# A trunk layer on one core, with a block of unused products and element-wise instructions behind its last product

## The chip, the core and the metric

The kernel runs on one core of one Trainium2 chip. A core has five engines, each with its own instruction queue: TensorE (PE in the profile; its weight loads are shown apart as PEld), VectorE (DVE), ScalarE (ACT), GpSimd (POOL) and SyncE (SP), which here issues the transfers. Engines wait for each other through semaphores. TensorE writes to PSUM, of which there are eight banks of 512 fp32 columns; all other data of the core lie in SBUF.

The metric is the device time of one execution in microseconds, as the median of the runs. A profile, taken in an execution of its own, gives the start and the duration of each instruction; its times count from the first instruction, and its span ends with the last one.

## What is computed

One layer of a diffusion backbone, for 128 context tokens and 512 latent tokens with the same weights: normalisation and modulation, attention and a short convolution as mixers, and a convolutional feed-forward network. What concerns us is its last line:

```python
def conv_ffn(u, p):
    up = dwconv3(u @ p["w_up"], p["conv_ffn"])
    g, val = jnp.split(up, 2, axis=-1)
    return (jax.nn.silu(g) * val) @ p["w_down"]

def trunk_layer(h, ada, p, rope_tabs, ctx_k, ctx_v):
    ...
    u = rms_norm(h, p["g_pre2"]) * (1 + sc2) + sh2
    h = h + g2 * rms_norm(conv_ffn(u, p), p["g_post2"])
    return h, k, v
```

`w_down` has 2816 rows and 1024 columns. Everything is fp32.

## The kernel before

**Products.** An fp32 operand is split into two parts, `hi` (the value rounded to fp32r, the shorter format that TensorE takes at the full rate) and `lo` (what is left). ScalarE writes `hi` with a copy, VectorE writes `lo` with a subtraction. A product is then three products on TensorE, hi x hi, hi x lo and lo x hi, which add up in one PSUM bank. `mm3` (lines 235 to 237) issues the three.

**The end of the kernel.** The last product is that of the activations with the right half of `w_down`'s columns. Its rows are taken in pairs of 128 (index `p`). The latent tokens go by a scheme of Strassen's kind with seven block products for each pair, which are added up in seven banks (`accs[1]` to `accs[7]`, function `part`); the 128 context tokens go directly (function `context`, into `pms[0]`). For the last three pairs (`held`) the block products are put in another order: first 1, 5, 6, 7 of all three pairs, then 4, then 2, then 3, and last the context tokens. While TensorE still works on the later ones, VectorE combines the finished banks to output rows (`u2`, `u3`, `u4`, `C1`, `C2`), ScalarE sums their squares (`second_half`), GpSimd or VectorE makes the factor of the normalisation, and `stored` (line 2368) scales the rows, adds the input `h` and has SyncE store them. The context tokens are the last product and the last rows to be stored.

**Who sets the order.** In this part each engine takes its instructions in the order in which the code is written, and a recording layer adds the semaphore waits: for the writer of what is read, for the readers and the writer of what is overwritten. Room in SBUF goes by tags: `raw_tile()` gives the next of three rooms of 128 x 1024 fp32, and its first writer waits for the last readers of the tile that lay there.

**Names that the change uses.** `AR[0]` and `AR[1]` are rooms of fp32 activations, free at the end but for `p1`, `u2`, `u3` and `u4`. `AL` and `AH` hold the `lo` and `hi` parts of the activations in fp32r. `SR` and `TR` are two rooms of 1024 columns each in the tile `RAWS`. `JK` is a place for results that nobody reads, `ssqs` holds sums and factors of one column each. `state["raw"][base + NPAIR - 1]` is the last piece of `w_down` as it was loaded. Banks 3, 4, 5 and 6 held `accs[7]`, `accs[1]`, `accs[5]` and `accs[6]`.

Of the kernel before, what the change touches and what calls it, by code (L numbers as in the profile page):

```python
# [14 lines left out]
F16 = mybir.dt.float16  # L15
BF16 = mybir.dt.bfloat16
I32 = mybir.dt.int32
AF = mybir.ActivationFunctionType
ALU = mybir.AluOpType
# [93 lines left out]
def trunk_layer(ctx, tc, x_prompt, x_sample, cache_k, cache_v, c, c_ctx, w_ada, b_ada, g_pre1, g_post1, g_pre2,  # L113
# [3 lines left out]
    V, S, G, PE = nc.vector, nc.scalar, nc.gpsimd, nc.tensor  # L117
# [10 lines left out]
    def yrows(t):  # L128
        return y_prompt if t == 0 else y_sample[(t - 1) * 128:t * 128, :]
# [14 lines left out]
    def nm(s):  # L144
        cnt[0] += 1
        return f"{s}_{cnt[0]}"

    def region(pool, tag, shape, dtype, name):
        return pool.tile([128] + shape, dtype, tag=tag, name=name)
# [30 lines left out]
    state = {"next": 0, "raw": [], "cut": [], "limit": 10}  # L180

    def raw_tile():
        return wp.tile([128, 1024], F32, tag="raw", name=nm("raw"), bufs=3)
# [190 lines left out]
    with tc.tile_pool(name="pro", bufs=2) as pro, tc.manual_schedule(engines={mybir.EngineType.SP}):  # L374
# [216 lines left out]
        raw = state["raw"][0][:, 0:512]  # L591
# [41 lines left out]
        for f in range(2, KT):  # L633
# [32 lines left out]
            if f == KT - 3:  # L666
                V.tensor_scalar(out=gains[0], in0=gains[0], scalar1=HD ** -0.5, scalar2=None, op0=ALU.mult)
                for i in range(2):
                    for a in range(2):
                        V.tensor_tensor(out=tabs[i][:, :, 0, a * 32:a * 32 + 32], in0=rt[:, :, 0, a * 32:a * 32 + 32],  # L670
                                        in1=gains[i][:, :, a * 32:a * 32 + 32].broadcast_to((128, 4, 32)), op=ALU.mult)
                        for hf in range(2):
                            d0, s0 = a * 32 + hf * 16, a * 32 + (1 - hf) * 16
                            V.tensor_tensor(out=tabs[i][:, :, 1, d0:d0 + 16], in0=rt[:, :, 1, d0:d0 + 16],
                                            in1=gains[i][:, :, s0:s0 + 16].broadcast_to((128, 4, 16)), op=ALU.mult)
            if f == KT - 2:
# [9 lines left out]
                                op0=ALU.mult)  # L686
# [3 lines left out]
    AH = Halves(NTOK, F32R, "AH")  # L690
    AL = region(ra, "r3", [KT, NTOK], F32R, "AL")
# [22 lines left out]
    def work(name, eng, do, after=(), rooms=()):  # L714
        works.append(Work(name, eng, do, list(after), list(rooms)))
        return works[-1]
# [30 lines left out]
    with tc.tile_pool(name="att", bufs=1) as at:  # L747
# [11 lines left out]
        ssqs = at.tile([128, 4, 4], F32, name="ssqs")  # L759
# [140 lines left out]
        for t in range(NT):  # L900
# [30 lines left out]
            h = work(f"k{t} hi", "ACT", k_hi, [tk], [pk])  # L931
# [47 lines left out]
        for i in range(3):  # L979
            a = work(f"v hi {i}", "ACT",  # L980
                     lambda i=i: S.activation(VH[:, 0, 2 * i:2 * i + 2, :], rooms_v[i].tmp(), AF.Copy), scaled, [rooms_v[i]])
# [71 lines left out]
        for n, (g, t, pi) in enumerate(steps):  # L1053
# [52 lines left out]
            else:  # L1106
                pts[n], exs = [], []
                for h in hs:
# [16 lines left out]
                    if h:  # L1125
# [3 lines left out]
                                                                                   accum_out=mk[:, 4 + h:5 + h]), [mx], [ar[h]] + [er] * way)  # L1129
# [43 lines left out]
            if pi in (None, 1):  # L1173
# [20 lines left out]
                r = work(f"R{n}", "ACT", spread, list(pvs), [pvr, xr])  # L1194
                o = work(f"O{n}", "DVE", whole, [r], [pvr, xr])
                a = work(f"AH{n}", "ACT", ah, [o], [pvr])
# [50 lines left out]
    def bank(i):  # L1247
        if i >= 2 and len(pools) == 1:
            early.close()
            pools.append(ctx.enter_context(tc.tile_pool(name="pb", bufs=1, space=bass.MemoryType.PSUM)))  # L1250
        return pools[i >= 2].tile([128, 512], F32, tag=f"b{i}", name=nm(f"b{i}"))
# [289 lines left out]
    for m, (x, i) in enumerate(PAIRS):  # L1541
# [10 lines left out]
        e, o = 2 * before[1] if m else 0, 2 * before[1] + 1 if m else 0  # L1552
# [666 lines left out]
    NPAIR, NP0 = NJ // 2 - 2, 1  # L2219
    A0 = region(ra, "r0", [4, 2 * NACT], F32R, "A0")  # L2220
    A1 = region(ra, "r1", [4, 2 * NACT], F32R, "A1")
    AL, AH = [A0[:, i, :] for i in range(3)], [A0[:, 3, :], A1[:, 0, :], A1[:, 1, :]]
    T2 = A1.rearrange("p i c -> p (i c)")[:, 4 * NACT:4 * NACT + 2048]
    A2 = ra.tile([128, 2, 2 * NACT], F32, tag="r2a", name="A2")
    AR = [A2[:, i, :] for i in range(2)]
    EX = region(rb, "r4", [NT, D], F32, "EX")
    GJ = rb.tile([128, 2560], F32, tag="r5a", name="GJ")
    G2, JK = GJ[:, 0:2048].rearrange("p (r c) -> p r c", r=2), GJ[:, 2048:2560]
    RAWS = rb.tile([128, 2560], F32, tag="r5b", name="RAWS")
    SR, TR, C22 = RAWS[:, 0:1024], RAWS[:, 1024:2048], RAWS[:, 2048:2560]  # L2230
    SS, TS = {}, {2: T2}
    ssqs = sm_.tile([128, NT, 2], F32, name="ssqs", bufs=1)
# [75 lines left out]
    def part(p, n):  # L2308

        u, x, y = state["cut"][base + p], s_room(p), t_room(p)  # L2310
        l, r = {1: lambda: (share(p, NACT + X1), u.at(1, 0, 256)), 2: lambda: (share(p, X1), u.at(0, 0, 256)),
                3: lambda: (summed(x, 3), u.at(0, 256, 256)), 4: lambda: (share(p, X2), summed(y, 3)),
                5: lambda: (summed(x, 0), summed(y, 1)), 6: lambda: (summed(x, 2), summed(y, 2)),
                7: lambda: (summed(x, 1), summed(y, 0))}[n]()
        if n not in accs:
            accs[n] = bank({1: DBANKS[2], 5: DBANKS[3], 6: DBANKS[4], 7: DBANKS[1]}[n])
        for t in range(2):
            ts = slice(t * 128, t * 128 + 128)
            mm3(accs[n][:, t * 256:t * 256 + 256], l[0][:, ts], l[1][:, ts], *r, p == NP0 and t == 0 and n in (1, 5, 6, 7), p == NPAIR - 1 and t == 1)
# [23 lines left out]
    def halves_of(x):  # L2343
        return x.rearrange("p (i c) -> p i c", i=2)

    def second_half(t, src):
        row = 1 if t == 0 else 0
        first, second = ssqs[:, t, 0:1], ssqs[:, t, 1:2]
        S.activation(halves_of(JK), src, AF.Square, accum_out=second)  # L2349
        if t == 0:  # L2350
            V.tensor_tensor(out=EX[:, t, 512:1024], in0=pms[0], in1=G2[:, row, 512:1024], op=ALU.mult)
            S.activation(second, second, AF.Sqrt, bias=first)
            V.reciprocal(second, second)
        else:
            G.tensor_tensor(out=second, in0=second, in1=first, op=ALU.add)  # L2355
            G.tensor_tensor(out=second, in0=second, in1=mhalf[:, 0:1], op=ALU.pow)
# [7 lines left out]
    def stored(t, n=1):  # L2364
        r = ssqs[:, t, 1:2]
        for i in range(n):
            cs = slice(i * D // n, (i + 1) * D // n)
            V.scalar_tensor_tensor(out=EX[:, t, cs], in0=EX[:, t, cs], scalar=r, in1=room["h"][:, t, cs], op0=ALU.mult, op1=ALU.add)
            nc.sync.dma_start(yrows(t)[:, cs], EX[:, t, cs])
# [22 lines left out]
    w, x, y = NJ - 3, NJ - 2, NJ - 1  # L2392
# [30 lines left out]
    base = state["next"]  # L2423
# [35 lines left out]
    for p in held:  # L2459
        if p + 2 < NPAIR:  # L2460
            prepared(p + 2)
        for n in (1, 5, 6, 7):
            part(p, n)
    S.activation(ssqs[:, 0, 1:2], mhalf[:, 0:1], AF.Sqrt, scale=-1.0)
    p1, u2, u3, u4 = (AR[i // 2 % 2][:, i % 2 * 512:i % 2 * 512 + 512] for i in (2, 3, 0, 1))
    S.activation(p1, accs[1], AF.Copy)
    minus(C22, C22, accs[5])
# [24 lines left out]
        stored(t, 2)  # L2492
    second_half(0, halves_of(pms[0]))
    stored(0, 2)
    fixed.close()


# [27 lines left out]
```

## Time and profile before

| | us |
|---|---|
| median of 2 runs | 1075.42 |
| the runs | 1075.06 and 1075.78 |
| span of the profiled execution | 1073.0 |
| TensorE busy in it | 1056.8 |
| VectorE busy | 899.9 |
| ScalarE busy | 598.4 |
| GpSimd busy | 133.1 |

The profiled execution has no time of its own beside its span; the two runs were taken apart from it. A busy time is the time in which an engine had at least one instruction under way. Instructions of one engine can overlap in the profile (a product is shown with its whole way through the array), so how many of a kind fit into a stretch is read from the distance of their starts.

Rows of the timeline read: start in us, duration in us, engine, line of the kernel, operation, output<-inputs, shapes, and xN where N equal instructions in a row are merged (their duration is then from the first start to the last end). Idle time ahead of an instruction stands in brackets with what ended it. Rows by line or by name read: count, then duration in ns as minimum/median/maximum, or busy us and mean ns.

### The profile page before, as it was taken

What the parts mean: (1) busy time and instruction counts of PE and PEld (TensorE: products, weight loads), DVE (VectorE), ACT (ScalarE), POOL (GpSimd) and SP (SyncE); (2) the same over time, 40 slices, a digit from 0 to 9 for tenths busy, and PEclk for the clock granted to TensorE, in tenths of its full rate; (3) what the DMA queues carried; (4) which work ended last, traced back from release to release, by engine and by line L of the source; (5) the groups of instructions that cost most, each with busy time, mean ns of one, the idle gap of its engine ahead of it and who ended that gap; (6) DMA issues with size and microseconds to landing.
All of it is one profiled execution on the core that took longest, in us unless ns stands there. A gap on an engine that the chain in (4) does not pass through costs nothing.

```text
span 1073.0 us, 20652 instructions
## 1 busy us (share of the span) xinstructions
PE 1056.8 (98%) x8216; PEld 995.4 (93%) x8216; DVE 899.9 (84%) x1379; ACT 598.4 (56%) x1057; POOL 133.1 (12%) x162
## 2 busy tenths in 40 slices
PE   8999999999999999999999999999999999999997
PEld 6788898899999999999998789999999999999996
DVE  5699999865498999896599678889999988989897
ACT  5478999942344544445322366645555555546673
POOL 1087676500000000000000020000000000000001
PEclk9999999999999999999999999999999999999999
DMA  9829999962244333223668634434544534436873
GB/s 320 256 82 175 190 168 187 191 147 60 75 123 124 93 103 94 79 79 99 189 188 253 198 131 129 121 116 136 166 131 152 150 122 131 152 116 219 277 275 115
DMA packets 243197, 164.02 MB, mean 153 GB/s; under 512 B 94874, under 2 KB 216214, under 8 KB 243102
## 3 DMA queue, kind: packets, MB, share of 16 engines
q1 hardware_dynamic: 242990, 162.68, 55.5%
q8 instruction: 64, 1.05, 0.4%
q14 instruction: 31, 0.25, 0.1%
q10 hardware_dynamic: 112, 0.04, 0.0%
HBM read 123.31 MB, written 17.36 MB: 131 GB/s over the span
## 4 chain that ended last, share of the span: by engine, by line
PE 90%; DVE 3%; ACT 2%; DMA 1%; POOL 1%; issue 1%; SPq 1%; DVEq 0%; ACTq 0%; POOLq 0%
PE b L1274 47%; PE b L235 10%; PE b L237 10%; PE b L236 9%; PE s L709 4%; PE s L1073 2%; PE s L1170 2%; PE s L235 1%; PE s L237 1%; PE s L1162 1%; PE s L478 1%; DVE marks L1120 1%; PE s L236 1%; PE b L1900 1%; ACT P L1134 1%
## 5 line engine op out<-in xcount | busy, mean ns | idle before, releaser
L1274 PE MATMUL b<-ZBr,whi 128*128 128x320 f32 x688 | 152.1, 309 | 0.0
L1274 PE MATMUL b<-MT,whi 128*128 128x320 f32 x608 | 134.4, 309 | 0.0
L1274 PEld LDWEIGHTS b<-ZBr,whi 128*128 128x128 f32 x688 | 114.9, 188 | 0.1
L1274 PE MATMUL b<-ZBr,wlo 128*128 128x320 f32 x344 | 106.1, 308 | 0.0
L1274 PEld LDWEIGHTS b<-MT,whi 128*128 128x128 f32 x608 | 101.7, 188 | 0.0
L1274 PE MATMUL b<-MT,wlo 128*128 128x320 f32 x304 | 94.0, 309 | 0.0
L1261 ACT ACTIVATE whi<-SUM 128x1024 fp32r<-128x1024 f32 x40 | 42.2, 1055 | 78.3 <-DVE SUM L1813 75.7
L1843 DVE SCALAR_TENSOR_TENSOR Y<-C,cffn,Y 128x642 f32<-128x642 f32 x88 | 77.9, 886 | 0.9
L1261 ACT ACTIVATE whi<-WB 128x1024 fp32r<-128x1024 f32 x38 | 40.2, 1058 | 55.5 <-DVE WB L1368 55.5
L1274 PE MATMUL b<-ZBT,whi 128*128 128x320 f32 x320 | 71.0, 308 | 0.0
L1274 PE MATMUL b<-UL,whi 128*128 128x320 f32 x228 | 70.8, 311 | 0.0
L1274 PE MATMUL b<-UH,wlo 128*128 128x320 f32 x228 | 70.1, 307 | 0.0
L1274 PE MATMUL b<-UH,whi 128*128 128x320 f32 x228 | 69.7, 306 | 0.0
L1282 ACT ACTIVATE p<-b 128x320 f32<-128x320 f32 x78 | 34.1, 437 | 55.3 <-PE b L1274 53.5
L1274 PEld LDWEIGHTS b<-ZBr,wlo 128*128 128x128 f32 x344 | 64.6, 188 | 0.0
L1265 DVE TENSOR_TENSOR wlo<-raw,whi 128x1024 fp32r<-128x1024 f32 (+1 forms) x51 | 50.4, 1020 | 13.4 <-ACT whi L1261 13.4
L1274 PEld LDWEIGHTS b<-MT,wlo 128*128 128x128 f32 x304 | 57.1, 188 | 0.0
L1274 PEld LDWEIGHTS b<-ZBT,whi 128*128 128x128 f32 x320 | 54.2, 188 | 1.6
L1120 DVE TENSOR_REDUCE marks<-s 128x1 f32<-128x640 f32 x64 | 52.1, 817 | 4.0 <-PE s L1073 3.8
L1265 DVE TENSOR_TENSOR wlo<-WB,whi 128x1024 fp32r<-128x1024 f32 x38 | 46.5, 1224 | 8.8 <-ACT whi L1261 8.7
L2355 POOL TENSOR_TENSOR ssqs<-ssqs 128x1 f32<-128x1 f32 x4 | 1.4, 356 | 412.9 <-ACT GJ L2349 412.9
L1261 ACT ACTIVATE whi<-raw 128x1024 fp32r<-128x1024 f32 (+1 forms) x51 | 43.5, 892 | 15.4 <-DMA raw<-in_w_o_dram 12.5
(477 smaller groups left out, 3348.1 us busy)
## 6 DMA issues: line engine op xcount, KB each, us to landing
raw<-in_w_in_dram SPq DMA_DIRECT2D x48, 512.0 KB
RAW<-in_w_up_dram SPq DMA_DIRECT2D x40, 512.0 KB
raw<-in_w_down_dram SPq DMA_DIRECT2D x22, 512.0 KB
GA<-in_w_ada_dram SPq DMA_DIRECT2D x16, 512.0 KB
actd<-Y SPq DMA_DIRECT2D x18, 321.0 KB
actl<-ACTb SPq DMA_DIRECT2D x18, 321.0 KB
A<-actl SPq DMA_DIRECT2D x9, 642.0 KB
A<-actd SPq DMA_DIRECT2D x9, 642.0 KB
```

Of the source, the lines that this page charges most:

```text
L235: PE.matmul(out, ah, bh, start=start, stop=False)
L236: PE.matmul(out, ah, bl, start=False, stop=False)
L237: PE.matmul(out, al, bh, start=False, stop=stop)
L709: PE.matmul(out, a, b, start=start and n == 0, stop=stop and n == 2, skip_group_check=True)
L1073: PE.matmul(o[h], q_of(hl, i, rows), kk[kx][rows, g, ks], start=m == 0, stop=m == 2, tile_position=(64 * h, 0), skip_group_check=True)
L1120: V.tensor_reduce(out=mk[:, h:h + 1], in_=s_of(), axis=AX.X, op=ALU.max, negate=True)
L1170: PE.matmul(p[64 * h:64 * h + 64, i * 128:i * 128 + 128], VH[:, w, s, vc_], src, start=k == 0 and m == 0, stop=k == ks[-1][0] and m == 2, ...
L1261: S.activation(to[0], raw, AF.Copy)
L1265: V.tensor_tensor(out=lo, in0=raw, in1=hi.bitcast(F32), op=ALU.subtract)
L1274: PE.matmul(out, p[:, ws], q[:, k, :], start=start and k == 0 and n == 0, stop=stop and k == 3 and n == 2, skip_group_check=True)
L1282: S.activation(t, pair[j][b], AF.Copy)
L1843: V.scalar_tensor_tensor(out=y, in0=crows(j)[i][:, d:d + NACT], scalar=cffn[:, 44 * d + o:44 * d + o + 1], in1=y, op0=ALU.mult, op1=ALU.add)
```

## The change

A block is added that computes nothing for the outputs.

Behind the first part of the held pairs, ScalarE fills a new tile of 16-bit numbers, `H16` (a `raw_tile()` seen as 2048 fp16 columns), with two copies of the last piece of `w_down`, scaled by 64.

Behind the last `stored`, TensorE gets 288 products, each written alone (`start` and `stop`) into one of four banks in turn:

- 168 fp16 products with weights and moving operand from `H16`: 48 of 320 columns, 24 of 512, 24 of 256, 30 of 160, 30 of 128 and 12 of 320 (the loops run `count // 3` times over three products)
- 48 fp32r products on `AL` and `AH`: 24 of 320 columns, 12 of 512, 12 of 256
- 48 fp16 products of 320 columns on half the array's rows, the two halves in alternation
- 24 fp32r products of the same kind

Then VectorE gets 25 instructions of 128 x 1024 elements on fp32 inputs, all but one with 16-bit results in `H16[:, 0:1024]`: four subtractions, four scaled subtractions, one subtraction into `SR` (fp32), twelve subtractions, and four multiplications by a factor per row. GpSimd gets four fp32 additions of `SR` into `TR`, beside the twelve subtractions. ScalarE gets three squares of 512 elements with a sum, and six copies of 1024 elements into `H16[:, 0:1024]`, three of them with a factor read from `ssqs`.

```diff
     S.activation(ssqs[:, 0, 1:2], mhalf[:, 0:1], AF.Sqrt, scale=-1.0)
+    H16 = raw_tile().bitcast(F16)
+    for i in range(2):
+        S.activation(H16[:, 1024 * i:1024 * i + 1024], state["raw"][base + NPAIR - 1], AF.Copy, scale=64.0)
     p1, u2, u3, u4 = (AR[i // 2 % 2][:, i % 2 * 512:i % 2 * 512 + 512] for i in (2, 3, 0, 1))
     S.activation(p1, accs[1], AF.Copy)
...
     second_half(0, halves_of(pms[0]))
     stored(0, 2)
+    pbank = [bank(b) for b in (4, 5, 6, 3)]
+    turns = [0]
+
+    def pmm(l, r, n, rows=None, x=None):
+        o = pbank[turns[0] % 4] if x is None else pbank[x]
+        turns[0] += 1
+        PE.matmul(o[:, 0:n], l, r, start=True, stop=True, skip_group_check=True, **({} if rows is None else dict(tile_position=(rows, 0))))
+
+    for n, count in ((320, 48), (512, 24), (256, 24), (160, 32), (128, 32), (320, 12)):
+        for i in range(count // 3):
+            w = [H16[:, (2 * i + a) % 4 * 128:(2 * i + a) % 4 * 128 + 128] for a in range(2)]
+            y = [H16[:, 512 + 512 * a:512 + 512 * a + n] for a in range(2)]
+            for a, c in ((0, 0), (0, 1), (1, 0)):
+                pmm(w[a], y[c], n)
+    for n, count in ((320, 24), (512, 12), (256, 12)):
+        for i in range(count // 3):
+            w = [AL[a][:, (2 * i + a) % 4 * 128:(2 * i + a) % 4 * 128 + 128] for a in range(2)]
+            y = [AH[a][:, 0:n] for a in range(2)]
+            for a, c in ((0, 0), (0, 1), (1, 0)):
+                pmm(w[a], y[c], n)
+    for i in range(24):
+        for h in range(2):
+            rows = slice(64 * h, 64 * h + 64)
+            pmm(H16[rows, i % 4 * 128:i % 4 * 128 + 128], H16[rows, 512:832], 320, 64 * h, 2 * (i // 3 % 2) + h)
+    for i in range(12):
+        for h in range(2):
+            rows = slice(64 * h, 64 * h + 64)
+            pmm(AL[0][rows, i % 4 * 128:i % 4 * 128 + 128], AH[0][rows, 0:320], 320, 64 * h, 2 * (i // 3 % 2) + h)
+    a0, a1 = AR[0][:, 0:1024], AR[1][:, 0:1024]
+    for i in range(4):
+        V.tensor_tensor(out=H16[:, 0:1024], in0=a0, in1=a1, op=ALU.subtract)
+    for i in range(4):
+        V.scalar_tensor_tensor(out=H16[:, 0:1024], in0=a0, scalar=ssqs[:, 0, 1:2], in1=a1, op0=ALU.mult, op1=ALU.subtract)
+    V.tensor_tensor(out=SR, in0=a0, in1=a1, op=ALU.subtract)
+    for i in range(4):
+        G.tensor_tensor(out=TR, in0=a0, in1=SR, op=ALU.add)
+    for i in range(12):
+        V.tensor_tensor(out=H16[:, 0:1024], in0=a0, in1=a1, op=ALU.subtract)
+    for i in range(4):
+        V.tensor_scalar(out=H16[:, 0:1024], in0=a0, scalar1=ssqs[:, 0, 1:2], scalar2=None, op0=ALU.mult)
+    for i in range(3):
+        S.activation(JK, a0[:, 0:512], AF.Square, accum_out=ssqs[:, 3, 0:1])
+    for i in range(3):
+        S.activation(H16[:, 0:1024], a0, AF.Copy)
+    for i in range(3):
+        S.activation(H16[:, 0:1024], a0, AF.Copy, scale=ssqs[:, 0, 1:2])
     fixed.close()
```

How the instructions then stand on the engines is shown at three places. The first is ScalarE behind the last split of the held pairs, where `raw_11853` is the new tile `H16`, `raw_11683` the loaded weights, `A` the room of `p1` and `b` the bank of `accs[1]`.

```order
 L2464 ACT_TABLE_LOAD
 L2464 ACTIVATE ssqs<-mhalf 128x1
-L2466 ACTIVATE A_11085<-b_895_11427 128x512 [waits PE_49,Activation_49]
+L2467 ACTIVATE raw_11853<-raw_11683 128x1024 [waits Activation_49]
+L2467 ACTIVATE raw_11853<-raw_11683 128x1024
+L2469 ACTIVATE A_11085<-b_895_11427 128x512 [waits PE_49,Activation_49]
 L2349 ACTIVATE GJ,ssqs<-RAWS 128x512 [waits DVE_49]
```

The two copies into `H16` stand ahead of the copy of `accs[1]`; the names in brackets are the engines whose semaphore is waited for.

The second is TensorE from the last product of the context tokens on, in the kernel with the change.

```order
L235 MATMUL b_877_11090<-whi_11765,A_11084 128x512
L236 MATMUL b_877_11090<-wlo_11766,A_11084 128x512
L237 MATMUL b_877_11090<-whi_11765,A_11083 128x512
L2504 LDWEIGHTS raw_11853 [waits Activation_49]
L2504 MATMUL b_916_11975<-raw_11853 128x320 [waits Activation_49]
L2504 LDWEIGHTS raw_11853 [waits DVE_49]
L2504 MATMUL b_917_11976<-raw_11853 128x320 [waits PE_49]
L2504 LDWEIGHTS raw_11853
L2504 MATMUL b_918_11977<-raw_11853 128x320 [waits PE_49]
```

The new products follow directly; an fp16 product has its weight load as an instruction of its own, and the waits are for the copies into `H16` and for the last readers and writers of the four banks.

The third is VectorE at the end of the program.

```order
 L2368 SCALAR_TENSOR_TENSOR EX<-EX,ssqs,HX 128x512 [waits DVE_49]
 L2368 SCALAR_TENSOR_TENSOR EX<-EX,ssqs,HX 128x512
-L2521 UNCONDITIONAL_BRANCH
+L2528 TENSOR_TENSOR raw_11853<-A_11085 128x1024 [waits PE_49]
+L2528 TENSOR_TENSOR raw_11853<-A_11085 128x1024 [waits DVE_49] x3
+L2530 SCALAR_TENSOR_TENSOR raw_11853<-A_11085,ssqs 128x1024 [waits DVE_49] x4
+L2531 TENSOR_TENSOR RAWS<-A_11085 128x1024
+L2535 TENSOR_TENSOR raw_11853<-A_11085 128x1024 [waits DVE_49] x12
+L2537 TENSOR_SCALAR raw_11853<-A_11085,ssqs 128x1024 [waits DVE_49] x4
+L2570 UNCONDITIONAL_BRANCH
```

The first subtraction waits for TensorE, that is for the last reader of `H16` among the products, and each one that writes `H16` waits for the one ahead of it. On ScalarE the first of the six copies into `H16` waits for VectorE's last multiplication in the same way; on GpSimd the first addition waits for the subtraction into `SR`, and each further one for the addition ahead of it. SyncE's queue has the same transfers as before.

## The prediction

> **What bounds the kernel now.** I read the busy shares and the clock first, then the timeline of the last 12 us, then the closing barrier, and then the rows from which each kind of added instruction can be priced.
>
> On the page, a busy share stands behind each engine, and the clock line has one digit for each fortieth of the span.
>
> ```profile
> PE 1056.8 (98%) x8216; PEld 995.4 (93%) x8216; DVE 899.9 (84%) x1379; ACT 598.4 (56%) x1057; POOL 133.1 (12%) x162
> PEclk9999999999999999999999999999999999999999
> ```
>
> TensorE is busy from end to end at the full clock, so whatever stands behind its last product starts when that product ends. The timeline of the end (start in us, duration in us, engine, line) shows that moment and what follows it.
>
> ```profile
> 1065.33 0.39 PE L236 MATMUL b<-wlo,A 128*128 128x512 f32 x1
> 1065.56 0.39 PE L237 MATMUL b<-whi,A 128*128 128x512 f32 x1
> 1067.61 0.68 DVE L2351 TENSOR_TENSOR EX<-b,GJ 128x512 f32<-128x512 f32 x1
> 1068.21 0.15 DVE L2353 RECIPROCAL ssqs<-ssqs 128x1 f32<-128x1 f32 x1
> 1068.39 1.42 DVE L2368 SCALAR_TENSOR_TENSOR EX<-EX,ssqs,HX 128x512 f32<-128x512 f32 x2
> ```
>
> The next product could start at 1065.56 + 0.23 = 1065.8 us, 0.23 us being the distance of the two rows. VectorE is done at 1069.8 us. Behind that lie the last store and a barrier of all engines, here by line, with the first and last start:
>
> ```profile
> L2521 SPq DRAIN  x3: 7/7/13, 1072.2 to 1072.5; - x3
> L2521 POOLq EVENT_SEMAPHORE  x4: 17/17/17, 1072.3 to 1072.9; - x4
> ```
>
> SyncE is the last to arrive, at 1072.2 us, and the span ends at 1073.0: 0.8 us from the last arrival to the end, whoever is last. The span is 1073.0 us; the two runs took 1075.06 and 1075.78 us, so 2.4 us of their median of 1075.42 lie around the span. I keep these 2.4 us and add only what the span grows by.
>
> **What the change puts on the path.** The added work is one chain over three engines. TensorE does 216 products that read the new 16-bit tile H16 (and 48 on fp32r operands among them). The first new subtraction of VectorE overwrites H16, so it waits for the last fp16 product; the 24 fp32r half-row products behind that are beside it (1.8 us at 0.147 a pair, below, if they were not). Each VectorE instruction that writes H16 waits for the one before. ScalarE's six copies write the same part of H16, so they wait for all of VectorE's. The three products, subtractions and copies thus add up, and nothing is left of the old kernel that could hide them: its stores are over by 1072.2 us, some 25 us before TensorE is through. No result is stored, so no DMA is added.
>
> **TensorE.** A product's price in a stream is the distance to the next one, not its duration.
>
> ```profile
> 63.55 0.82 PE L947 MATMUL s<-P,some 128*128 128x256 bf16 x6
> L947 PEld LDWEIGHTS <-some x6: 98/98/98, 63.4 to 64.0; 128*128 128x128 bf16 x6
> L947 PE MATMUL s<-P,some x6: 272/272/273, 63.6 to 64.1; 128*128 128x256 bf16 x6
> 634.50 0.60 PE L1748 MATMUL b<-ident,TX 128*128 128x128 f32 x4
> L1748 PEld LDWEIGHTS b<-ident,TX x40: 138/140/145, 620.4 to 648.8; 128*128 128x128 f32 x40
> 329.83 0.31 PE L1274 MATMUL b<-MT,whi 128*128 128x320 f32 x1
> ...
> 330.86 0.31 PE L1274 MATMUL b<-MT,wlo 128*128 128x320 f32 x1
> 1061.38 0.28 PE L236 MATMUL b<-wlo,SS 128*128 128x256 f32 x1
> 1061.50 0.28 PE L237 MATMUL b<-whi,SS 128*128 128x256 f32 x1
> 84.40 0.31 PE L1073 MATMUL s<-KL,QT 64*128 64x320 f32 x2
> 84.55 0.46 PE L1073 MATMUL s<-KH,QT 64*128 64x320 f32 x4
> 84.84 0.31 PE L1073 MATMUL s<-KL,QT 64*128 64x320 f32 x2
> ```
>
> The kernel has no fp16 product over the whole array, but six bf16 ones of 256 columns, each with its own weight load like the new ones: (0.82 - 0.27) / 5 = 0.110 us apart. fp32r products of 256 columns are 0.12 us apart, those of 320 columns 1.03 / 7 = 0.147 us (seven steps between the two rows), those of 512 columns 0.23. Taking the bf16 row by columns, fp16 costs 0.1375 us at 320 columns and 0.220 at 512: 60 x 0.1375 + 24 x 0.220 + 24 x 0.110 = 16.2 us.
>
> For the 30 products of 160 and the 30 of 128 columns the columns alone would give 0.069 and 0.055 us, and then the weight load may be the limit. The f32 products of 128 columns are (0.60 - 0.27) / 3 = 0.109 us apart although their columns need half of that, so there the load is the limit. A 16-bit load is shown 42 ns shorter than an f32 one (98 against 140 ns). I take 0.109 - 0.042 = 0.067 us as its limit: 30 x 0.069 + 30 x 0.067 = 4.1 us, between 3.7 (columns alone) and 6.5 us (the f32 limit).
>
> On such loads the Trainium skill says two things. "TensorE: Matmul & The Clock Gate", in its section LDWEIGHTS, gives columns divided by 1.2 GHz, 107 ns for 128 columns, and by it the 60 narrow products would cost 6.4 us and the total 2.3 us more; a whole bf16 load shown with 98 ns speaks against it. The section on fast weight load of the same page has 16-bit loads of 128 columns at about twice the speed, and the shorter bf16 load of this trace agrees in direction.
>
> The 48 fp32r products cost 24 x 0.147 + 12 x 0.23 + 12 x 0.12 = 7.7 us. The 48 fp16 half-row products run as pairs: the trace has such pairs (each x2) 0.44 / 3 = 0.147 us apart, so 24 x 0.147 = 3.5 us. Sum: 16.2 + 4.1 + 7.7 + 3.5 = 31.5 us, until 1097.3. The last product ends 0.31 us after its start and not 0.147, which with a signal makes 1097.5 us. If fp16 were as slow as fp32r at every width, it would be 60 x 0.0095 + 24 x 0.011 + 24 x 0.010 + 2.4 = 3.5 us more.
>
> **VectorE.** These rows give its instructions of 1024 elements, and one that writes 16-bit results.
>
> ```profile
> L2261 DVE TENSOR_TENSOR SS<-RAWS,SS x8: 1217/1221/1231, 1009.3 to 1051.0; 128x1024 fp32r<-128x1024 f32 x8
> L1141 DVE SCALAR_TENSOR_TENSOR P<-s,P 128x640 f16<-128x640 f32 x32 | 26.2, 820 | 2.7 <-ACT P L1134 2.4
> L342 DVE SCALAR_TENSOR_TENSOR GA<-GA,s,GA x28: 1276/1280/1285, 532.9 to 601.6; 128x1024 f32<-128x1024 f32 x28
> L440 DVE TENSOR_SCALAR xn<-XT,rstd x5: 744/753/753, 6.8 to 13.3; 128x1024 f32<-128x1024 f32 x5
> ```
>
> A 16-bit result gains nothing: 0.82 us for 640 elements would be 1.31 for 1024, not less than the 1.22 of a 32-bit one. I take 1.22, since a fixed part is in the 0.82. A wait for the instruction before adds about 0.035 us (RECIPROCAL above ends at 1068.36, the next starts at 1068.39). So 17 subtractions x 1.255 = 21.3, 4 scaled subtractions x 1.315 = 5.3, 4 multiplications x 0.79 = 3.1: 29.7 us alone. The multiplications have twice the rate in the row, with a 32-bit result; if that is lost, 4 x 0.47 = 1.9 us come on top.
>
> **GpSimd beside it.** Its four additions of 1024 elements meet the last twelve subtractions. Two places in the trace show such a meeting; the lines of L831 give the undisturbed and the longest case.
>
> ```profile
> L831 POOL TENSOR_TENSOR wlo<-raw,whi x13: 1271/1289/1805, 71.2 to 193.6; 128x512 fp32r<-128x512 f32 x13
> L831 DVE TENSOR_TENSOR wlo<-raw,whi x5: 681/693/1221, 112.0 to 189.8; 128x512 fp32r<-128x512 f32 x5
> 112.01 1.82 DVE L831 TENSOR_TENSOR wlo<-raw,whi 128x512 fp32r<-128x512 f32 x2
> 112.24 1.04 POOL L870 TENSOR_TENSOR QF<-QF,X 128x256 f32<-128x256 f32 x1 [0.18 <-DVE QF L850]
> 152.37 0.69 DVE L831 TENSOR_TENSOR wlo<-raw,whi 128x512 fp32r<-128x512 f32 x1
> 152.41 1.80 POOL L831 TENSOR_TENSOR wlo<-raw,whi 128x512 fp32r<-128x512 f32 x1 [2.19 <-ACT whi L826]
> L1139 POOL TENSOR_TENSOR P<-E,P 128x640 f16<-128x640 f32 x29 | 40.8, 1408 | 30.3 <-ACT P L1134 30.2
> ```
>
> At 152.4 us VectorE started first; GpSimd's instruction ended 1.15 us after VectorE's (154.21 against 153.06), nearly its whole undisturbed 1.29. At 112 us GpSimd's ended at 113.28, and VectorE's second subtraction, which takes 0.69 undisturbed, was stretched to 1.22 and ended at 113.83, 0.55 us behind it. So two such instructions take turns, and a turn saves 0.14 us on either side. In the new block VectorE leaves a gap of 0.035 us between two subtractions, in which a waiting addition gets its turn, and each addition waits for the one before, so VectorE goes ahead once in between: four turns. An addition of 1024 elements is 2.25 us by the 1.41 of 640 elements and 2.58 by the 1.29 of 512; I take 2.4. Four turns cost VectorE 4 x (2.4 - 0.28) = 8.5 us, between 0 (no turns) and 9.2 (2.58 each). The additions end within the twelve subtractions. The Trainium skill, "SBUF — State Buffer", section on who interferes with whom, calls this an exclusive lock in which the loser fully blocks; both places above agree. VectorE's part: 29.7 + 8.5 = 38.2 us, until 1135.7.
>
> **ScalarE.** The three squares of 512 elements follow its last old instruction and are hidden under TensorE's 31 us (uncovered, at least 3 x 0.60 us, as the 512 elements at 1053.33 below). The six copies come last.
>
> ```profile
> 1049.53 1.04 ACT L2258 ACTIVATE SS<-RAWS 128x1024 fp32r<-128x1024 f32 x1
> L1134 ACT ACTIVATE P<-E x29: 728/738/780, 80.5 to 209.6; 128x640 f16<-128x640 f32 x29
> L1838 ACT ACTIVATE Y<-C,cffn x44: 816/830/842, 681.7 to 985.7; 128x642 f32<-128x642 f32 x44
> 1051.88 0.20 ACT L2464 ACTIVATE ssqs<-mhalf 128x1 f32<-128x1 f32 x1
> 1053.33 0.60 ACT L2466 ACTIVATE A<-b 128x512 f32<-128x512 f32 x1 [1.25 <-PE b L237]
> 1054.77 0.69 DVE L1288 TENSOR_TENSOR A<-A,b 128x512 f32<-128x512 f32 x1
> ```
>
> A copy takes 1.05 us; one with a scale read from SBUF about 0.1 us more (0.83 against 0.74 at some 640 elements). With 0.04 us for each wait: 3 x 1.09 + 3 x 1.19 = 6.8 us, and 0.1 us for the signal: until 1142.6. The two copies that fill H16 stand ahead of the copy of accs[1] (1053.33). They take 2.1 us from 1052.1, so that copy starts at 1054.2 and ends at 1054.8, when the subtraction that reads it starts (1054.77). That costs under 0.1 us, and TensorE waits for none of it.
>
> **Sum.** 1142.6 + 0.8 = 1143.4 us of span, 70.4 more than 1073.0. With the median of the runs: 1075.4 + 70.4 = 1146 us, slower by 6.5%.
>
> **The rivals.**
> - *No turns.* GpSimd's additions cost VectorE nothing, because they run beside it or wait until it is through. The first gives 1146 - 8.5 = 1137 us. In the second the additions (9.6 us) run beside the copies (6.8 us) and end 2.8 us later: 1140 us. For it: the two places have single meetings, none has a train of them. Against it: both show the later one waiting.
> - *Dearer instructions.* fp16 no faster than fp32r (+3.5), no double rate with a 16-bit result (+1.9), longer additions (+0.7), 1.31 us for a 16-bit subtraction (17 x 0.09 = +1.5): up to 1153 us. The bf16 row and the weight-load rows speak against the largest of these.
> - *Not slower.* The results are read by nobody, and if the build drops instructions without a reader, nothing but the copies into H16 and no time is left: 1075 us. It decides from the point where less than 28.7 us stand behind the last product (within 2% is up to 1073.0 + 21.5 = 1094.5 us of span). The rows of the changed program have all 288 products, so I give it next to nothing; even if all engines worked side by side without the chain, TensorE's 33 us would pass that point.
>
> **Chances.** The sum as worked out 0.65, no turns 0.18, dearer 0.15, not slower 0.02. The likeliest is 1146 us. The range runs from the lowest rival of the slower side, 1137 less 1 for narrow products at the rate of their columns, to 1152, where most of the dearer case is inside. A measurement of this kernel can tell about 2% from no change; every case but the last is 5 to 7% slower, so 0.98 slower, 0.01 the same, 0.01 faster.
>
> **What the changed profile would show.** TensorE's new line starts at 1065.8 and its fp16 parts end near 1097.5; VectorE's first subtraction waits for TensorE there. If the turns are right, four of the twelve subtractions are some 2 us longer than the others and GpSimd's additions are spread over the first five or six of them; if not, all twelve are 1.22 us. The last instruction is a copy of ScalarE, and the span ends 0.8 us behind it. Wrong would be: narrow products at 0.11 us, multiplications at 1.22 us, or a VectorE that starts long before TensorE's fp16 parts are through.

## The result, and the profile after

The kernel with the block takes 1143.93 us (median of 2 runs, 1143.71 and 1144.16) against 1075.42 us before: 1.064 times as long, with a 95% interval of 1.061 to 1.067. The profiled execution has a span of 1141.9 us, 68.9 us more than the 1073.0 before; the median lies 2.0 us above it.

The busy shares on the page of the kernel after:

```profile
PE 1089.5 (95%) x8504; PEld 1020.8 (89%) x8504; DVE 936.5 (82%) x1404; ACT 609.2 (53%) x1071; POOL 146.1 (13%) x166
```

TensorE has 288 products more (8504 against 8216), and unlike before it is not busy to the end. The timeline of the kernel after, from the old kernel's last product on (start in us, duration in us, engine, line; xN are merged):

```profile
1065.36 0.39 PE L237 MATMUL b<-whi,A 128*128 128x512 f32 x1
1065.59 19.87 PE L2504 MATMUL b<-raw 128*128 128x320 f16 x168
...
1085.19 0.42 PE L2504 MATMUL b<-A 128*128 128x320 f32 x1
1085.45 0.31 PE L2504 MATMUL b<-A,A 128*128 128x320 f32 x1
...
1087.19 0.31 PE L2504 MATMUL b<-A,A 128*128 128x320 f32 x1
...
1093.10 3.43 PE L2504 MATMUL b<-raw 64*128 64x320 f16 x48
1096.26 2.03 PE L2504 MATMUL b<-A 64*128 64x320 f32 x24
1096.57 5.01 DVE L2528 TENSOR_TENSOR raw<-A 128x1024 f16<-128x1024 f32 x4 [26.96 <-PE b L2504]
1101.61 5.25 DVE L2530 SCALAR_TENSOR_TENSOR raw<-A,ssqs 128x1024 f16<-128x1024 f32 x4
1106.78 1.22 DVE L2531 TENSOR_TENSOR RAWS<-A 128x1024 f32<-128x1024 f32 x1
1107.91 23.15 DVE L2535 TENSOR_TENSOR raw<-A 128x1024 f16<-128x1024 f32 x12
1108.13 13.04 POOL L2533 TENSOR_TENSOR RAWS<-A,RAWS 128x1024 f32<-128x1024 f32 x4 [42.22 <-issue]
1131.10 3.12 DVE L2537 TENSOR_SCALAR raw<-A,ssqs 128x1024 f16<-128x1024 f32 x4
1134.31 3.23 ACT L2541 ACTIVATE raw<-A 128x1024 f16<-128x1024 f32 x3 [65.33 <-DVE raw L2537]
1137.57 3.51 ACT L2543 ACTIVATE raw<-A,ssqs 128x1024 f16<-128x1024 f32 x3
```

It is one staircase: each engine starts where the one ahead of it is done. VectorE had been idle for 26.96 us when the last fp16 product let it go, and ScalarE for 65.33 us when VectorE did. GpSimd's additions start 0.2 us behind the first of the twelve subtractions. The end of the program is the same as before, 0.8 us from the last arrival to the end; here ScalarE's last copy ends at 1141.08 and the barrier's events of GpSimd run to

```profile
L2570 POOLq EVENT_SEMAPHORE  x4: 17/17/17, 1141.3 to 1141.8; - x4
```

The terms of the sum, in us:

| | forecast | measured |
|---|---|---|
| first new product | 1065.8 | 1065.6 |
| 168 fp16 products | 20.3 | 19.60 (1065.59 to 1085.19) |
| 48 fp32r products | 7.7 | 7.91 (to 1093.10) |
| 48 fp16 half-row products | 3.5 | 3.16 (to 1096.26) |
| VectorE's first subtraction | 1097.5 | 1096.57 |
| VectorE's part | 38.2 | 37.65 (to 1134.22) |
| ScalarE's copies, with the signal | 6.9 | 6.86 (to 1141.08) |
| to the end of the span | 0.8 | 0.8 |

Two boundaries in this table need care. These rows of TensorE are the last fp16 products ahead of the fp32r ones, the last fp32r product, and forty of the half-row products (twenty pairs):

```profile
1084.89 0.57 PE L2504 MATMUL b<-raw 128*128 128x320 f16 x3
1092.88 0.28 PE L2504 MATMUL b<-A 128*128 128x256 f32 x1
1093.38 2.88 PE L2504 MATMUL b<-raw 64*128 64x320 f16 x40
```

The last fp16 product starts at 1084.89 + 2 x 0.135 = 1085.16, so the first fp32r product is shown only 0.03 us behind it and the second another 0.26 us later: together the 0.28 us of an fp16 and an fp32r step. Some 0.1 us of the 7.91 thus belong to the 19.60. In the same way the last half-row pair is followed after 0.03 us by the next product, so the 3.16 us hold one step less than the 24 pairs. Within the row the pairs are (2.88 - 0.30) / 19 = 0.136 us apart, 0.30 us being the last product's duration.

The chain that ended last, in order of time, shows the twelve subtractions one by one (start, time on the chain; the first six are printed):

```profile
1107.99 1.15 DVE raw L2535
1109.17 3.26 DVE raw L2535
1112.45 3.26 DVE raw L2535
1115.72 3.26 DVE raw L2535
1119.00 3.25 DVE raw L2535
1122.28 1.24 DVE raw L2535
```

The second to the fifth take 3.26 us and all behind them 1.24: four turns of 2.02 us, as long as GpSimd has additions left. The durations by line say the same from both sides (count, minimum/median/maximum in ns):

```profile
L2535 DVE TENSOR_TENSOR raw<-A x12: 1219/1226/3246, 1107.9 to 1129.8; 128x1024 f16<-128x1024 f32 x12
L2533 POOL TENSOR_TENSOR RAWS<-A,RAWS x4: 3198/3200/3202, 1108.1 to 1118.0; 128x1024 f32<-128x1024 f32 x4
```

### The profile page after: what moved, and what is told of

It reads as the page before. It is cut to its first block, busy times and chain, and to the rows that moved or that the text cites. A ratio compares the mean times of both kernels' runs of the same rounds, so it can differ in the third digit from the quotient of the medians.

```text
span 1141.9 us, 21273 instructions
## 1 busy us (share of the span) xinstructions
PE 1089.5 (95%) x8504; PEld 1020.8 (89%) x8504; DVE 936.5 (82%) x1404; ACT 609.2 (53%) x1071; POOL 146.1 (13%) x166
## 4 chain that ended last, share of the span: by engine, by line
PE 90%; DVE 5%; ACT 2%; POOL 1%; DMA 1%; issue 1%; SPq 0%; ACTq 0%; DVEq 0%; POOLq 0%
PE b L1274 45%; PE b L235 9%; PE b L237 9%; PE b L236 9%; PE s L709 4%; PE b L2504 3%; PE s L1073 3%; PE s L1170 2%; DVE raw L2535 2%; PE s L1162 1%; PE s L235 1%; PE s L237 1%; PE s L478 1%; PE s L236 1%; PE b L1900 1%
```

## The experiments

The theory was a chain TensorE, VectorE, ScalarE that adds up, with turns between VectorE and GpSimd. The rivals were that VectorE is held or stretched by something else. All changes are made to the kernel after. The old part of the kernel ended up to 0.8 us earlier or later from one execution to the next (the first new product started between 1065.6 and 1066.4 us), so parts of the block are compared by their lengths where it matters: from VectorE's first subtraction to ScalarE's last copy, 44.51 us in the kernel after (1096.57 to 1141.08).

**Without the additions.**

```diff
-    for i in range(4):
-        G.tensor_tensor(out=TR, in0=a0, in1=SR, op=ALU.add)
```

> The four additions of GpSimd are left out. Turns theory (an addition and a subtraction with both inputs in SBUF exclude each other, each addition stretches one subtraction from 1.22 to 3.25 us): all twelve subtractions take 1.22 us and the span falls by 4 x 2.02 = 8.1 us, from 1141.9 to 1133.8 us. Rival (the long subtractions come from something else, as the waits of VectorE on itself or the 16-bit results): four of the twelve stay at 3.25 us and the span at 1141.9 us.

Measured: 1135.79 us, span 1134.1 us. The twelve subtractions by line, with the shortest, the middle and the longest in ns:

```profile
L2533 DVE TENSOR_TENSOR raw<-A x12: 1219/1224/1226, 1108.2 to 1122.1; 128x1024 f16<-128x1024 f32 x12
```

The first piece of the block in the timeline, VectorE's last and ScalarE's last (start and length in us):

```profile
1096.88 5.00 DVE L2528 TENSOR_TENSOR raw<-A 128x1024 f16<-128x1024 f32 x4 [26.96 <-PE b L2504]
...
1123.32 3.12 DVE L2535 TENSOR_SCALAR raw<-A,ssqs 128x1024 f16<-128x1024 f32 x4
...
1129.79 3.51 ACT L2541 ACTIVATE raw<-A,ssqs 128x1024 f16<-128x1024 f32 x3
```

Not one subtraction is over 1.226 us. The part from 1096.88 to 1133.30 is 36.42 us, 8.09 less than with the additions. So the long subtractions are the additions' doing, and the rival falls.

**Eight additions.**

```diff
-    for i in range(4):
+    for i in range(8):
         G.tensor_tensor(out=TR, in0=a0, in1=SR, op=ALU.add)
```

> Eight additions of GpSimd instead of four. Turns theory: eight of the twelve subtractions take 3.25 us, one addition between each two, and the span grows by 4 x 2.02 = 8.1 us to 1150.0 us. Rival (VectorE wins the later meetings and keeps going): the subtractions behind the fifth stay at 1.22 us, the last additions end beside ScalarE's copies, and the span stays within 3 us of 1141.9 us.

Measured: 1152.27 us, span 1150.9 us. The median of the subtractions is now the long one. The rows by line, then the first and the last piece of the block in the timeline:

```profile
L2535 DVE TENSOR_TENSOR raw<-A x12: 1216/3245/3247, 1108.8 to 1138.8; 128x1024 f16<-128x1024 f32 x12
L2533 POOL TENSOR_TENSOR RAWS<-A,RAWS x8: 3196/3201/3204, 1109.0 to 1131.9; 128x1024 f32<-128x1024 f32 x8
```

```profile
1097.41 5.01 DVE L2528 TENSOR_TENSOR raw<-A 128x1024 f16<-128x1024 f32 x4 [26.96 <-PE b L2504]
...
1146.50 3.51 ACT L2543 ACTIVATE raw<-A,ssqs 128x1024 f16<-128x1024 f32 x3
```

Eight of twelve subtractions are stretched, the second to the ninth, and the part grows to 52.60 us, 8.09 more than with four. The turns are strict: in this train neither engine gets two in a row while the other waits.

**The second input from PSUM.** The twelve subtractions read a bank, 512 columns twice, in place of `a1`.

```diff
+    b1 = pbank[0].unsqueeze(1).broadcast_to((128, 2, 512))
     for i in range(12):
-        V.tensor_tensor(out=H16[:, 0:1024], in0=a0, in1=a1, op=ALU.subtract)
+        V.tensor_tensor(out=H16[:, 0:1024].rearrange("p (i c) -> p i c", i=2), in0=a0.rearrange("p (i c) -> p i c", i=2), in1=b1, op=ALU.subtract)
```

> The twelve subtractions read their second input from a PSUM bank (512 columns, read twice) instead of from SBUF; the four additions stay. Turns over the second SBUF input: no subtraction is stretched, each takes 1.22 to 1.3 us, the additions run beside them at 2.2 to 2.4 us each, and the span falls by some 8 us to 1133 to 1135 us. Rival (turns between any VectorE and GpSimd instructions of this size, or over the write side): four subtractions stay near 3.2 us and the span near 1141.9 us.

Measured: 1135.71 us, span 1134.2 us.

```profile
L2536 DVE TENSOR_TENSOR raw<-A,b x12: 1215/1221/1222, 1108.3 to 1122.1; 128x1024 f16<-128x1024 f32 x12
L2533 POOL TENSOR_TENSOR RAWS<-A,RAWS x4: 2343/2345/2347, 1108.5 to 1115.8; 128x1024 f32<-128x1024 f32 x4
```

Both run at their own pace in the same stretch of time: 1.22 us for a subtraction and 2.35 for an addition, which is taken here as its undisturbed length (no run has the additions without VectorE beside them). The 3.20 us shown for an addition in the kernel after would then hold some 0.85 us of waiting. What the additions and these subtractions take turns over is the second SBUF input, not SBUF as a whole and not the write.

**Multiplications beside the additions.** The additions are moved behind the twelve subtractions, ahead of twelve multiplications by a factor per row, which read one tile from SBUF beside the factor and run at twice the rate.

```diff
-    V.tensor_tensor(out=SR, in0=a0, in1=a1, op=ALU.subtract)
-    for i in range(4):
-        G.tensor_tensor(out=TR, in0=a0, in1=SR, op=ALU.add)
     for i in range(12):
         V.tensor_tensor(out=H16[:, 0:1024], in0=a0, in1=a1, op=ALU.subtract)
-    for i in range(4):
+    V.tensor_tensor(out=SR, in0=a0, in1=a1, op=ALU.subtract)
+    for i in range(4):
+        G.tensor_tensor(out=TR, in0=a0, in1=SR, op=ALU.add)
+    for i in range(12):
         V.tensor_scalar(out=H16[:, 0:1024], in0=a0, scalar1=ssqs[:, 0, 1:2], scalar2=None, op0=ALU.mult)
```

> The subtraction into SR and the four additions stand behind the twelve subtractions, and twelve multiplications (one SBUF input, 0.753 us each, which is twice the rate of a subtraction) follow beside them instead of four. Turns over the shared pair of ports, which a double-rate instruction takes too: the subtractions take 1.22 us, four multiplications are stretched by some 2 us each, and the span is 1141.9 + 8 x 0.79 = 1148.2 us. Rival (only a second SBUF input excludes GpSimd): no multiplication is stretched and the span is 1148.2 - 8.1 = 1140.1 us.

Measured: 1150.00 us, span 1148.4 us. The multiplications in the timeline, then they and the additions by line:

```profile
1123.41 17.25 DVE L2537 TENSOR_SCALAR raw<-A,ssqs 128x1024 f16<-128x1024 f32 x12
L2537 DVE TENSOR_SCALAR raw<-A,ssqs x12: 746/754/2711, 1123.4 to 1139.9; 128x1024 f16<-128x1024 f32 x12
L2535 POOL TENSOR_TENSOR RAWS<-A,RAWS x4: 2665/2667/2727, 1123.6 to 1131.9; 128x1024 f32<-128x1024 f32 x4
```

Four multiplications, the second to the fifth, go from 0.75 to 2.71 us, a turn of 1.96 us each; twelve undisturbed ones would take some 9.4 us in place of 17.25 (four take 3.12 in the kernel after). So turns also come with one tile read from SBUF, where the subtraction with one SBUF input and one from PSUM had none. The multiplication differs from that one in its double rate, but also in the factor that it reads from SBUF, and no run parts the two. That the double rate is the reason is what the section on who interferes with whom of the Trainium skill's page "SBUF — State Buffer" says of such instructions, and this trace agrees with it.

**A tile of their own.** The results of VectorE and ScalarE go into a second 16-bit tile, so that nothing of theirs waits for TensorE.

```diff
+    Q16 = raw_tile().bitcast(F16)
     a0, a1 = AR[0][:, 0:1024], AR[1][:, 0:1024]
     for i in range(4):
-        V.tensor_tensor(out=H16[:, 0:1024], in0=a0, in1=a1, op=ALU.subtract)
+        V.tensor_tensor(out=Q16[:, 0:1024], in0=a0, in1=a1, op=ALU.subtract)
...
```

> The 16-bit results of VectorE and ScalarE go into a tile of their own instead of the one that TensorE reads. Chain theory: VectorE starts at 1069.6 us, right behind its last old instruction, its part of 37.7 us ends at 1107.3 and ScalarE's copies at 1114.2, beside TensorE, which ends at 1098.3 as now; the span falls by 27 us to 1115.0 us. Rival (VectorE was held by something else, or runs slower beside TensorE's products): the span stays at 1141.9 us in the first case, in the second it falls by under 24 us.

Measured: 1117.40 us (1.039 times the time before, 1.038 to 1.041), span 1115.7 us. The timeline:

```profile
1070.18 5.00 DVE L2529 TENSOR_TENSOR raw<-A 128x1024 f16<-128x1024 f32 x4
...
1081.52 23.34 DVE L2536 TENSOR_TENSOR raw<-A 128x1024 f16<-128x1024 f32 x12
1081.73 13.22 POOL L2534 TENSOR_TENSOR RAWS<-A,RAWS 128x1024 f32<-128x1024 f32 x4 [15.16 <-issue]
...
1096.92 2.03 PE L2504 MATMUL b<-A 64*128 64x320 f32 x24
1104.89 3.12 DVE L2538 TENSOR_SCALAR raw<-A,ssqs 128x1024 f16<-128x1024 f32 x4
...
1111.30 3.51 ACT L2544 ACTIVATE raw<-A,ssqs 128x1024 f16<-128x1024 f32 x3
```

VectorE starts right behind its last old instruction, runs beside TensorE's 31 us, and the end comes 26.2 us earlier. Its part is 37.8 us long (1070.18 to 1108.01) against 37.65 alone, with the difference in the turns (23.34 against 23.15 us), and TensorE's products kept their distances. One overwritten tile was worth 26 of the 69 us.

**Narrow products.**

```diff
-    for n, count in ((320, 48), (512, 24), (256, 24), (160, 32), (128, 32), (320, 12)):
+    for n, count in ((320, 48), (512, 24), (256, 24), (96, 32), (64, 32), (320, 12)):
...
-    for n, count in ((320, 24), (512, 12), (256, 12)):
+    for n, count in ((320, 24), (512, 12), (128, 12)):
```

> The 30 fp16 products of 160 columns get 96 columns, the 30 of 128 get 64, and the 12 fp32r products of 256 columns get 128. Theory of the weight load (a 16-bit load of 128 columns takes the time that 128 columns take, about 0.055 us, and an fp32r load 0.109): 96 and 64 columns both stay at 0.053 to 0.057 us from product to product, fp32r falls from 0.117 only to 0.109. Rival (the columns alone set the pace down to 64): 0.043 us at 96 columns, 0.029 at 64. The limit of 0.067 us that was forecast for fp16 has already been undercut by 0.056 at 128 columns.

Measured, in one run: 1142.39 us, span 1140.5 us. The first of these rows is of the kernel after (128 columns), the others of this one (96 and 64 columns of fp16, 128 of fp32r):

```profile
1082.22 1.39 PE L2504 MATMUL b<-raw 128*128 128x128 f16 x22
```

```profile
1080.41 1.06 PE L2504 MATMUL b<-raw 128*128 128x96 f16 x21
1081.63 0.75 PE L2504 MATMUL b<-raw 128*128 128x64 f16 x20
...
1090.60 0.28 PE L2504 MATMUL b<-A 128*128 128x128 f32 x1
1090.71 0.27 PE L2504 MATMUL b<-A,A 128*128 128x128 f32 x1
```

The view of durations by line of the same kernel, with the shortest, the middle and the longest in ns, gives the length of the 64-column product as its shortest:

```profile
L2504 PE MATMUL b<-raw x216: 192/296/379, 1065.9 to 1094.8; 128*128 128x320 f16 x30, 64*128 64x320 f16 x24, 128*128 128x96 f16 x15, 128*128 128x64 f16 x15
```

With some 0.22, 0.21 and 0.19 us for the last product of each row, the distances are 1.17 / 21 = 0.056, 0.85 / 20 = 0.043 and 0.56 / 19 = 0.029 us. They follow the columns down to 64; the weight load of 128 columns sets no limit there, against the theory that went into this run. For fp32r something does: 0.11 us at 128 columns, which by its step at wider products would be about 0.06. The load is a likely cause, since the prediction's f32 products of 128 columns stood 0.109 us apart too; it is not shown, as no run has such narrow fp32r products with a shorter load.

**Half as many weight columns for fp32r.**

```diff
-        PE.matmul(o[:, 0:n], l, r, start=True, stop=True, skip_group_check=True, **({} if rows is None else dict(tile_position=(rows, 0))))
+        PE.matmul(o[0:l.shape[1], 0:n], l, r, start=True, stop=True, skip_group_check=True, **({} if rows is None else dict(tile_position=(rows, 0))))
...
-            w = [AL[a][:, (2 * i + a) % 4 * 128:(2 * i + a) % 4 * 128 + 128] for a in range(2)]
+            w = [AL[a][:, (2 * i + a) % 4 * 128:(2 * i + a) % 4 * 128 + 64] for a in range(2)]
```

> The 48 fp32r products over the whole array take 64 weight columns instead of 128, so that a weight load is half as long. They stood 0.147, 0.232 and 0.117 us apart at 320, 512 and 256 columns, where fp16 stood 0.136, 0.216 and 0.109 us apart. Theory A (the 32-bit moving operand itself streams 7 to 8% slower): the distances stay. Theory B (the 32-bit weight load beside it slows the stream): they fall halfway or all the way to the fp16 distances, 0.141 or less at 320 columns.

Measured, in one run: 1144.35 us, span 1142.6 us. The weight loads by line (shortest, middle and longest in ns), first of the kernel after, then of this one:

```profile
L2504 PEld LDWEIGHTS b<-A,A x16: 187/188/192, 1085.3 to 1092.7; 128*128 128x128 f32 x16
```

```profile
L2504 PEld LDWEIGHTS b<-A,A x16: 134/134/138, 1085.9 to 1093.3; 128*64 128x64 f32 x16
```

The loads are shown 0.054 us shorter. The rows of the 320-column products:

```profile
1086.81 0.31 PE L2504 MATMUL b<-A 128*64 128x320 f32 x1
...
1088.41 0.31 PE L2504 MATMUL b<-A 128*64 128x320 f32 x1
```

Eleven steps lie between the two: 1.60 / 11 = 0.145 us. In the kernel after, twelve steps between 1085.45 and 1087.19 (above) give the same 0.145. At these widths the length of the weight load does not make fp32r slower than fp16; theory B falls.

**fp16 columns 4 bytes apart.** The moving operand takes every second fp16 column.

```diff
-            y = [H16[:, 512 + 512 * a:512 + 512 * a + n] for a in range(2)]
+            y = [H16[:, 512 + 512 * a:512 + 512 * a + 2 * n:2] for a in range(2)]
```

> The moving operand of the 168 fp16 products takes every second column, so that 320 columns lie 4 bytes apart as those of fp32r do (0.147 us from product to product against 0.136 of dense fp16). Theory A1 (the stream is slowed by the 4 bytes that lie between two columns in SBUF): 0.147 us at 320 columns, 0.232 at 512, 0.117 at 256, and the block 1.1 us longer or more. Theory A2 (the fp32r format itself is slower): the distances stay at 0.136, 0.216 and 0.109 us and the block keeps its length.

Measured, in one run: 1145.18 us, span 1143.4 us. The first row is of the kernel after, the second of this one, each within the first 48 products of 320 columns:

```profile
1066.82 3.42 PE L2504 MATMUL b<-raw 128*128 128x320 f16 x24
```

```profile
1066.82 3.42 PE L2504 MATMUL b<-raw 128*128 128x320 f16 x23
```

In the same 3.42 us one product fewer fits: with 0.30 us for the last, 3.12 / 23 = 0.136 and 3.12 / 22 = 0.142 us. Neither theory holds alone. If the spacing acts on fp32r as it does on fp16, it makes 0.006 of the 0.010 us by which an fp32r product of 320 columns takes longer; the rest was not settled. The format itself is a candidate. Either way fp32r, on which the whole kernel counts as the format at the full rate, ran 7% below fp16 here (0.145 against 0.136 us).

## Why the prediction was right

The forecast was 1146 us; 1143.9 came. The steps one by one:

- *One chain that adds up, hidden by nothing.* Right, and shown by the tile of their own: with the one dependency gone, the end comes 26.2 us earlier, with the parts at their lengths.
- *TensorE's start and prices.* Right to 3%: 30.7 us against 31.5. Taking fp16 from the bf16 row by columns gave 0.1375 and 0.220 us, and 0.136 and 0.216 were measured. Two terms were mis-sized. The limit of 0.067 us for narrow products, made from the difference of two weight-load durations, does not exist; 128 columns take 0.056, which is 0.3 us less over 30 products. The half-row pairs were priced at fp32r's 0.147 us and stood 0.136 apart, as far as fp16 products of 320 columns over the whole array, which is another 0.3 us.
- *fp32r at the rows' distances.* Right: 7.9 against 7.7 us. Of the 0.2 us more, some 0.1 belong to the last fp16 product, as said below the table, and 0.1 stand at the change from fp32r to the half rows, where two starts are 0.22 us apart (1092.88 and 1093.10) in place of 0.12.
- *VectorE's prices.* Right: 29.6 us alone (1096.88 to 1126.44 without the additions) against 29.7. A 16-bit result changed nothing, neither for the subtractions (1.225 us) nor for the double rate of the multiplications (0.753).
- *Four turns.* Right in number and place. In size a turn was 2.02 us and not 2.12: an addition beside the PSUM subtractions is 2.35 us and was taken as 2.4, and a turn then saves 0.33 us of it in place of 0.28; why it does is not shown. The rival without turns, which had 0.18, fell in both its forms: the additions neither run beside the subtractions nor wait until these are through.
- *ScalarE's copies.* Right: 1.056 us, and 1.147 with a factor read from SBUF, against 1.05 and 1.15.
- *The two copies ahead of* `accs[1]`. Hidden, as said: the last old product started at 1065.36 us against 1065.56 before, and VectorE's last old instruction ended at 1069.6 against 1069.8.
- *From the span to the runs.* The median lay 2.0 us above the span of the profiled execution instead of 2.4. Both figures set the median beside the span of one execution; in the runs for which time and span of the same execution are on record, 1.7 to 1.9 us lie around it.

Of the 2 us between forecast and result, 1.5 are in the span and 0.4 here. Nearly every term came out a little short and only fp32r's a little long, so the hit does not rest on errors that cancel.

The dearer case fell with the prices of fp16, of the multiplications, of the additions and of the 16-bit subtractions, the one of dropped instructions with the 288 products in the trace.

## What to carry to other kernels

To price a new instruction, take the distance between starts in a stream of the nearest kind, not its duration, and scale that by columns; the worst price here was a limit made from two durations that overlap other work. Work on three engines that reuses one tile adds up as if it were on one engine, so look for the overwritten tile before the busy engine. Before putting GpSimd beside VectorE, look at what VectorE reads: here the additions cost nothing beside subtractions with one input from PSUM, and 1.96 to 2.02 us each, nearly their own 2.35, beside subtractions with two SBUF inputs and beside multiplications at the double rate.

## What the runs showed of the hardware that was not expected

- A 16-bit weight load of 128 columns, shown with 98 ns, sets no pace down to products of 64 columns 0.029 us apart, while fp32r products of 128 columns stay 0.11 us apart. The Trainium skill's page "TensorE: Matmul & The Clock Gate" gives in its section LDWEIGHTS columns divided by 1.2 GHz, which is 107 ns for 128 columns; for these fp16 loads the measurement decides against that. Its section on fast weight load has about twice the speed as measured, which is an estimate of some 53 ns; 0.029 us leaves no room for that either, if each load must fit between two products.
- Two fp16 products on half the array's rows each, one on either half, stand 0.136 us apart from pair to pair, as one product of 320 columns over the whole array does.
- fp16 columns read 4 bytes apart stream 4% slower than dense ones (0.142 against 0.136 us at 320 columns).
- Where both take two inputs from SBUF, GpSimd's additions and VectorE's subtractions alternate strictly over a train of instructions, eight times out of eight, at a constant 2.02 us a turn; with TensorE's products beside them the twelve subtractions take 0.2 us longer (23.34 against 23.15).
